# The first mixing of a two-layer network, rebuilt: four-pass products, another order of tiles, masks on the evicted product, long convolution and context FFN behind the recurrence

## The chip, the core and the metric

The kernel runs on one core of a Trainium2 chip. The time is the device time of one execution in microseconds. Before the change three executions took 2928.12, 2919.17 and 2926.59 us; the median is 2926.59. The engines are named as in the profile: PE is TensorE with PEld for its weight loads, DVE is VectorE, ACT is ScalarE, POOL is GpSimd, SP is SyncE, which issues the transfers.

## What is computed

One sequence of 256 tokens with 1024 features, and a context of 256 tokens. Cut to the part that the change touches, the reference does this:

```python
u = rmsnorm(x, mix_norm) @ w_in0                 # 1024 -> 3328 columns
y_r = rwkv7_bidir(u[..., :1792], ...)            # 8 heads of 64, both directions, a scan over 256 steps
y_h = hyena_bidir(u[..., 1792:], ...)            # long convolution through FFTs of 512 points
x = x + concat([y_r, y_h]) @ w_o0                # 512 + 512 -> 1024
# of the second block, which needs nothing of the first mixing:
mod = silu(cond) @ w_mod                         # shift, scale and gate vectors
ctx = ctx + gate * half_ffn(modulated_norm(ctx)) # the context's first half FFN
# then two convolved FFNs, two embeddings, a neighbourhood attention, and the rest of the second block
```

In the recurrence the state of a head is 64 x 64. At each step it is multiplied by a decay, loses its product with a key, and gains an outer product of value and key.

## The kernel before

All is kept feature major: 128 features on the partitions, 256 tokens along the free axis, eight such tiles for H, the residual stream.

A **product** of the kind `gemm` (L351 to L359) is done in three parts. ACT rounds a weight tile to a high part `wh` (L348), DVE or POOL subtracts it from the tile to make the low part `wl` (L349), and the activations are split alike. Each tile of 128 contracted features then has three products of 128x256 in fp32r: high by high (L357), low by high (L358), high by low (L359). Products with fp32 operands that are not split exist too, in the filters and transforms of the long convolution (L763, L783) and in the recurrence. The trace records such a product twice.

**First mixing** (`mix`, L792). The projection takes 26 tiles of columns, eight tiles of the contraction each, in the order of the columns: 0 to 3, 4 to 7 and 8 to 11 for the recurrence's r, k and v by quarter, 12 for decay and rate, 13 for the gate, 14 to 25 for the long convolution. Beside it run the modulation's tiles (`mod_until`, L897): a tile `wm` is 512 KB, DVE sums its product with one conditioning vector (L920), POOL multiplies it with the other (L924) and ACT sums that (L925); 24 tiles are done in the mixing, with two buffers. After tile 13 the first quarter of the recurrence is prepared. Then come the filters of the convolution (their net is three small layers with a Sin each, L704 to L714), the convolution, the solution of the first quarter, the context's norm, and for j = 1 to 3 `prepare(j)` and `solve(j)`. Last are the two halves of the output product (`out0`): the convolution's half is added to H behind the convolution, the recurrence's half at the end (L884).

**A quarter of the recurrence** is two heads in both directions, in eight chunks of 64 steps. `prepare` (L1437) makes decays, keys and values. `solve` (L1514) forms the products G inside the chunks, inverts I + N in blocks of 1, 2, 4 to 32, carries the states along the chunks, and makes the outputs. In the inversion X is the inverse and Y its transpose. Each level multiplies G by the level's mask (L1564, on POOL, one operation for each head's 64 partitions, into `Lv`), forms Lv times X by sixteen 64x64 products (L1557) that ACT copies to `Tm` (L1569), and from two more such batches DVE subtracts in X and Y (L1574, L1575). The first level makes Y and X from the mask alone (L1566, L1567). Behind the last level ACT copies the product that starts the states, W (L1578). Tiles carry the tags `a` and `b` in turn, by quarter.

**The context's first half FFN** needs only the modulation and the context. It is a generator (`half_ffn_on`) that gives its products the tag `fill`. Four of its steps belong to the mixing, the others are handed out after the next phases. Its `wl` is made on POOL as long as the tag is `fill` (L347).

The program is written as Python loops. A scheduler with a timeline model then fixes the order of instructions on each engine when the program is built; transfers marked with `keep_in_program_order` keep theirs. Each engine runs its own list in order, and waits for semaphores of the others. Behind the mixing follow `ffn0`, whose first products are those of L368 to L370 with the tag `mm`, then `ple0` and the rest, in both programs alike.

## Time and profile before

| | before |
|---|---|
| median of three executions | 2926.59 us |
| profiled execution, its span | 2921.7 us |
| PE, DVE, ACT, POOL busy | 95%, 69%, 44%, 24% |
| mean granted TensorE clock | 0.959 |
| traffic | 415.95 MB, 142 GB/s |

The profiled execution is not one of the three that are timed; its span, from the first to the last instruction, stands 4.9 us below their median. "Granted clock" is the share of full speed that PE had in a stretch. A timeline row gives the start, the length, the engine, the line, the operation, what it writes and reads, the size, how many were put together, and in brackets the idle time before it with what ended it. A row of the waits names the waiting instruction, what released it, the sum, how often, and the longest.

The whole span in 40 slices of 73 us, in tenths, shows that the first seven slices differ from the rest:

```
PE   7868999899999989999989999999999999999999
DVE  8896553689977689877764777764756555567555
POOL 3565655322541431241220101000010000121100
PEclk9878999899999999989999999999999999999999
```

### The profile page before, as it was taken

What the parts mean: (1) busy time and instruction counts of PE and PEld (TensorE: products, weight loads), DVE (VectorE), ACT (ScalarE), POOL (GpSimd) and SP (SyncE); (2) the same over time, 40 slices, a digit from 0 to 9 for tenths busy, and PEclk for the clock granted to TensorE, in tenths of its full rate; (3) what the DMA queues carried; (4) which work ended last, traced back from release to release, by engine and by line L of the source; (5) the groups of instructions that cost most, each with busy time, mean ns of one, the idle gap of its engine ahead of it and who ended that gap; (6) DMA issues with size and microseconds to landing.
All of it is one profiled execution on the core that took longest, in us unless ns stands there. A gap on an engine that the chain in (4) does not pass through costs nothing.

```text
span 2921.7 us, 49795 instructions
## 1 busy us (share of the span) xinstructions
PE 2763.4 (95%) x19770; PEld 2453.5 (84%) x19770; DVE 2010.3 (69%) x3432; ACT 1283.4 (44%) x2241; POOL 694.1 (24%) x448
## 2 busy tenths in 40 slices
PE   7868999899989999989999999999999999999999
PEld 6647888799889899989998669888898888895999
DVE  8896553689977689877764764777756555567555
ACT  5433322465645566555554453322233222355543
POOL 3565655322541431241220101000010000121100
PEclk9878999899999999989999999999999999999999
DMA  6421112466555376546641203665535444240554
GB/s 233 154 95 59 55 57 77 160 232 211 174 156 169 104 232 207 179 159 222 213 145 62 65 15 113 195 193 176 167 109 166 139 140 136 76 121 30 169 186 144
DMA packets 145882, 415.95 MB, mean 142 GB/s; under 512 B 31009, under 2 KB 49074, under 8 KB 144754
## 3 DMA queue, kind: packets, MB, share of 16 engines
q1 hardware_dynamic: 144930, 407.52, 43.8%
q0 software_dynamic: 720, 5.24, 0.5%
q8 instruction: 156, 2.56, 0.4%
q14 instruction: 76, 0.62, 0.1%
HBM read 411.66 MB, written 1.05 MB: 141 GB/s over the span
## 4 chain that ended last, share of the span: by engine, by line
PE 64%; DVE 5%; ACT 2%; issue 1%; POOL 0%; DMA 0%; SPq 0%; ACTq 0%; DVEq 0%; POOLq 0%
PE mm L359 17%; PE mm L357 17%; PE mm L358 17%; PE mm L1309 2%; PE mm L369 2%; PE mm L370 2%; PE mm L368 1%; DVE wl L349 1%; PE mm L1277 1%; PE aux L421 1%; PE aux L1303 1%; ACT wh L348 1%; PE fill L359 1%; PE fill L357 1%; PE fill L358 0%
## 5 line engine op out<-in xcount | busy, mean ns | idle before, releaser
L348 ACT CAST wh<-raw 128x1024 fp32r<-128x1024 f32 (+4 forms) x694 | 643.7, 935 | 1011.2 <-PE mm L358 569.2
L349 DVE TENSOR_TENSOR wl<-raw,wh 128x1024 fp32r<-128x1024 f32 (+4 forms) x552 | 690.3, 1254 | 292.6 <-ACT wh L348 283.7
L359 PE MATMUL mm<-xnh,wl 128*128 128x256 f32 (+1 forms) x2592 | 819.0, 316 | 2.1 <-DVE wl L349 2.1
L357 PE MATMUL mm<-xnh,wh 128*128 128x256 f32 (+1 forms) x2592 | 818.3, 316 | 0.7 <-ACT wh L348 0.7
L358 PE MATMUL mm<-xnl,wh 128*128 128x256 f32 (+1 forms) x2592 | 816.2, 315 | 0.0
L359 PEld LDWEIGHTS mm<-xnh,wl 128*128 128x128 f32 x2592 | 488.1, 188 | 35.7 <-DVE wl L349 3.2
L357 PEld LDWEIGHTS mm<-xnh,wh 128*128 128x128 f32 x2592 | 487.8, 188 | 35.7 <-issue 2.3
L358 PEld LDWEIGHTS mm<-xnl,wh 128*128 128x128 f32 x2592 | 487.8, 188 | 34.0
L358 PE MATMUL mm<-ml,wh 128*128 128x256 f32 (+1 forms) x1104 | 341.0, 311 | 6.7 <-DVE ml L349 6.7
L359 PE MATMUL mm<-mh,wl 128*128 128x256 f32 (+1 forms) x1104 | 341.3, 312 | 0.0
L357 PE MATMUL mm<-mh,wh 128*128 128x256 f32 (+1 forms) x1104 | 338.6, 312 | 0.5 <-ACT mh L348 0.5
L349 POOL TENSOR_TENSOR wl<-raw,wh 128x1024 fp32r<-128x1024 f32 (+3 forms) x142 | 257.2, 1819 | 296.9 <-ACT wh L348 246.4
L920 DVE CUSTOM_DVE_ANT_0 junk<-wm,sc,vecs 128x1024 bf16<-128x1024 f32 x224 | 292.2, 1304 | 6.1 <-DMA wm<-w_mod 2.5
L458 POOL TENSOR_TENSOR ss<-ss,xt 128x256 f32<-128x256 f32 x68 | 68.1, 1006 | 917.3 <-issue 690.0
L924 POOL TENSOR_TENSOR wm<-wm,sc 128x1024 f32<-128x1024 f32 x64 | 176.0, 2750 | 438.4 <-DVE mod L920 335.5
L358 PEld LDWEIGHTS mm<-ml,wh 128*128 128x128 f32 x1104 | 207.8, 188 | 21.0 <-DVE ml L349 7.9
L359 PEld LDWEIGHTS mm<-mh,wl 128*128 128x128 f32 x1104 | 207.4, 188 | 12.3
L357 PEld LDWEIGHTS mm<-mh,wh 128*128 128x128 f32 x1104 | 205.6, 188 | 13.2 <-ACT mh L348 0.9
L1003 DVE SCALAR_TENSOR_TENSOR H<-mm,mod,H 128x256 f32<-128x256 f32 x112 | 53.7, 482 | 116.8 <-PE mm L359 116.7
L1050 DVE TENSOR_TENSOR sg<-sg,mm 128x256 f32<-128x256 f32 (+1 forms) x88 | 48.7, 553 | 123.1 <-PE mm L359 120.8
L369 PE MATMUL mm<-xnl,wh 128*128 128x256 f32 x416 | 121.9, 300 | 7.9 <-DVE xnl L954 4.6
L370 PE MATMUL mm<-xnh,wl 128*128 128x256 f32 x416 | 120.2, 296 | 0.0
(539 smaller groups left out, 4738.3 us busy)
## 6 DMA issues: line engine op xcount, KB each, us to landing
raw<-s_up SPq DMA_DIRECT2D x220, 512.0 KB, 3.7
wm<-w_mod SPq DMA_DIRECT2D x144, 512.0 KB, 4.4
raw<-f_up SPq DMA_DIRECT2D x88, 512.0 KB, 4.5
raw<-s_dn SPq DMA_DIRECT2D x65, 512.0 KB, 3.6
raw<-w_in SPq DMA_DIRECT2D x60, 512.0 KB, 3.8
raw<-s_dn SPq DMA_DIRECT2D x60, 384.0 KB, 3.2
raw<-w_o SPq DMA_DIRECT2D x32, 512.0 KB, 3.7
raw<-f_dn SPq DMA_DIRECT2D x32, 512.0 KB, 4.2
```

Of the source, the lines that this page charges most:

```text
L348: self.nc.scalar.copy(hi, src)
L349: (self.nc.gpsimd if pool or self.tag == "fill" else self.nc.vector).tensor_sub(lo, src, hi.bitcast(F32))
L357: nc.tensor.matmul(out, wh[:, ws], h, start=first and k == 0, stop=False)
L358: nc.tensor.matmul(out, wh[:, ws], l, start=False, stop=False)
L359: nc.tensor.matmul(out, wl[:, ws], h, start=False, stop=last and k == kt - 1)
L369: nc.tensor.matmul(out, wh[:, s], l, start=False, stop=False)
L370: nc.tensor.matmul(out, wl[:, s], h, start=False, stop=k == kt - 1)
L458: nc.gpsimd.tensor_add(self.ss[s], self.ss[s], x)
L920: self.tc.keep_in_program_order(nc.vector.tensor_tensor_reduce(out=junk, in0=w, in1=self.sc[:, i], scale=0.5 if self.half else 1.0, scalar ...
L924: nc.gpsimd.tensor_mul(w, w, self.sc[:, 1])
L1003: nc.vector.scalar_tensor_tensor(self.HH[s][:, m], ps[:, c], gt, self.HH[s][:, m], op0=ALU.mult, op1=ALU.add)
L1309: nc.tensor.matmul(po[64 * h : 64 * h + 64, :T], v(k0 // P + i), pTs[h][:, i], start=i == 0, stop=i == nk // P - 1)
```

## The change

- The projection and the output product are no longer split. [...]
- The projection follows what the recurrence needs: tiles 12, 4, 0, 8, then `prepare(0)`, 13, `solve(0)`, then 5, 1, 9, `prepare(1)`, then all others; the filter net is written before the projection, the filters after it. Then `solve(1)`, quarters 2 and 3, the convolution with its half of the output, and the other half.
- The level mask multiplies the product as DVE evicts it (L1600 of the changed file); G itself goes into the product. POOL's masks and ACT's copy are gone.
- In `prepare` five operations go from POOL to DVE. The low parts in the mixing's fill come from DVE.
- Modulation, the context's norm and the context's FFN stand behind the recurrence and the output. For the modulation's 24 tiles both sums run on DVE (`aid=False`).
- The pool `nrm` has three buffers in place of two; the comments are gone, so line numbers differ.

The core of the diff:

```diff
-        (self.nc.gpsimd if pool or self.tag == "fill" else self.nc.vector).tensor_sub(lo, src, hi.bitcast(F32))
+        (self.nc.gpsimd if pool or self.own and self.tag == "fill" else self.nc.vector).tensor_sub(lo, src, hi.bitcast(F32))
...
+    def plain(self, out, w, kt, x):
+        for k in range(kt):
+            self.nc.tensor.matmul(out, w[:, k * P : (k + 1) * P], x[:, k], start=k == 0, stop=k == kt - 1)
...
-                        order = list(range(14)) + [14 + 4 * j + q for q in range(4) for j in range(3)]
-                        for t, wh, wl in self.wtiles("w_in0", order, KT):
...
-                            self.gemm(ps, wh, wl, KT, xh, xl)
...
-                            if t > 1:
-                                self.mod_until(t//3)
...
+                        net = self.filter_net(yp)
...
+                        project([12, 4, 0, 8])
+                        ready = prepare(0)
+                        project([13])
+                        solve(0, ready)
+                        project([5, 1, 9])
+                        ready = prepare(1)
+                        project([6, 2, 10, 7, 3, 11] + [14 + 4 * j + q for q in range(4) for j in range(3)])
+                        kr, ki, hn = self.filters(hp, yp, *net)
+                    rk.pools.append(self.pool(e2, "rke"))
+                    solve(1, ready)
+                    for j in range(2, 4):
+                        solve(j, prepare(j))
+                    self.tag = self.aux = "fill"
+                    self.hyena(x0, sv, kr, ki, hn)
+                self.out0(0, y)
+                fp = self.pool(ef, "fill", side="right")
+                with ExitStack() as e3:
+                    self.mod_open(self.pool(e3, "mod", side="right"), aid=False, eng=nc.sync)
                     self.mod_until(12)
...
+                nc.sync.dma_start(self.HH[1], self.ap["ctx"])
                 for k in range(KT):
                     self.sq_add(k, 1)
                 normed = self.norm2(fp, 0, 0, [1])
...
-        nc.gpsimd.tensor_scalar(lw, lw, 1.0, -0.5 * DECAY, op0=ALU.add, op1=ALU.mult)
+        nc.vector.tensor_scalar(lw, lw, 1.0, -0.5 * DECAY, op0=ALU.add, op1=ALU.mult)
...
-        for lev in range(6):
-            lv = t(pool, [P, 8, 64], "Lv", bufs=2)
-            for h, p in enumerate(PAR):
-                m = self.lmask[p, lev * 64 : lev * 64 + 64].unsqueeze(1).to_broadcast([64, 8, 64])
-                nc.gpsimd.tensor_mul(lv[p], G[p, :, h, 0:64], m)
...
-            nc.scalar.copy(Tm, batch(lambda u, h: lv[PAR[h], u], lambda u, h: X[PAR[h], u]))
+        for lev in range(1, 6):
+            m = self.lmask[:, lev * 64 : lev * 64 + 64].unsqueeze(1).to_broadcast([P, 8, 64])
+            nc.vector.tensor_mul(Tm, batch(lambda u, h: G[PAR[h], u, h, 0:64], lambda u, h: X[PAR[h], u]), m)
```

The order on the engines, at three places. First PE at the start of the program, before; `xnh` and `xnl` are the split norm, `a` the sums of the projection:

```order
L416 MATMUL b_137<-c_sums_64,x_27_120 128x2 x4
L442 MATMUL b_160<-c_ident_66,rsyb_147 128x128 x2
L357 MATMUL a_203<-xnh_163,wh_199 128x256
L357 MATMUL a_235<-xnh_163,wh_231 128x256
L358 MATMUL a_203<-xnl_164,wh_199 128x256
L359 MATMUL a_203<-xnh_163,wl_200 128x256
```

And PE at the same place now; L718 is the filter net, `hy` its layers, L381 the plain product, L1487 belongs to `prepare(0)`:

```order
L438 MATMUL fill_151<-c_sums_64,x_32_131 128x2 x4
L464 MATMUL fill_174<-c_ident_66,rsyfill_161 128x128 x2
L718 MATMUL fill_190<-feat_188,hw_186 64x256
L718 MATMUL fill_202<-hy_192,hw_186 64x256
L718 MATMUL fill_214<-hy_204,hw_186 64x256
L381 MATMUL fill_228<-xn_177,raw_226 128x256 x8
L381 MATMUL fill_240<-xn_177,raw_238 128x256 x8
L381 MATMUL fill_252<-xn_177,raw_250 128x256 x8
L1487 MATMUL b_297<-wa_274,wdec_281 128x256
```

The three products of the filter net stand ahead of the first plain product, and the recurrence's preparation follows after three tiles of the projection.

PE in the levels of a middle quarter, before; `fill` is the context's FFN, L1557 a batch of the inversion:

```order
L357 MATMUL fill_4185<-xnh_2249,wh_4188 128x256
L1557 MATMUL a_2617<-xyt_2459 64x64 x16
L1557 MATMUL a_2634<-xyt_2459 64x64 x16
L358 MATMUL fill_4185<-xnl_2250,wh_4188 128x256
L359 MATMUL fill_4185<-xnh_2249,wl_4189 128x256
L1557 MATMUL a_2656<-xyt_2459,Lv_2653 64x64 x16
```

And in the same levels now; L1586 is the batch, L1631, L1620 and L1624 the states of the quarter ahead, L381 the output product of the convolution:

```order
L1586 MATMUL b_1989<-xyt_1966,G_1918 64x64 x6
L381 MATMUL fill_3086<-sr_3019,raw_3084 128x256 x4
L381 MATMUL fill_3092<-sr_3019,raw_3084 128x256 x4
L1620 MATMUL a_1698<-S_1683,ar_987 64x64 x4
L1586 MATMUL b_2007<-xyt_1966 64x64 x16
L1586 MATMUL b_2024<-xyt_1966 64x64 x3
L1624 MATMUL a_1699<-Lv_1664,xyt_1389 64x64 x4
L1586 MATMUL b_2024<-xyt_1966 64x64 x13
L381 MATMUL fill_3100<-sr_3019,raw_3098 128x256 x3
```

Where the context's FFN stood between the batches, the states of the quarter ahead and the convolution's output stand now.

DVE at the end of the mixing, before; `H` with `a` is the last half of the output product, L386 the root of H's norm:

```order
L884 TENSOR_TENSOR H_59<-H_59,a_5282 128x256
L884 TENSOR_TENSOR H_59<-H_59,a_5303 128x256
L884 TENSOR_TENSOR H_59<-H_59,a_5326 128x256
L349 TENSOR_TENSOR wl_5394<-raw_5391,wh_5393 128x1024
L884 TENSOR_TENSOR H_59<-H_59,a_5347 128x256
L349 TENSOR_TENSOR wl_5406<-raw_5403,wh_5405 128x1024
L386 TENSOR_SCALAR rsxaux_5420<-aux_5415 128x2
```

And DVE there now; L949 is the reduce of a modulation tile `wm`, two for each tile:

```order
L913 TENSOR_TENSOR H_59<-H_59,fill_3155 128x256
L913 TENSOR_TENSOR H_59<-H_59,fill_3164 128x256
L349 TENSOR_TENSOR wl_3463<-raw_3460,wh_3462 128x1024
L913 TENSOR_TENSOR H_59<-H_59,fill_3175 128x256
L913 TENSOR_TENSOR H_59<-H_59,fill_3184 128x256
L949 ISA junk_3203,mod_73<-wm_3201,sc_3198,vecs_58 128x1024
L949 ISA junk_3205,mod_73<-wm_3201,sc_3198,vecs_58 128x1024
L949 ISA junk_3209,mod_73<-wm_3207,sc_3198,vecs_58 128x1024
L949 ISA junk_3211,mod_73<-wm_3207,sc_3198,vecs_58 128x1024
```

The modulation's reduces, which stood among the rows of the projection, follow the last add to H. 32 of them come before the rows of the context's norm, 16 stand between these.

## Rows read from the trace of the kernel before

**Rows 1.** Timeline of PE: start us, us, engine, line, operation, out<-in, count
```profile
561.83 0.28 PE L358 MATMUL fill<-xnl,wh 128*128 128x256 f32 x1
561.95 0.52 PE L368 MATMUL mm<-xnh,wh 128*128 128x256 f32 x3
```

**Rows 2.** Page, engines: busy us, share of the span, instructions
```profile
PE 2763.4 (95%) x19770; PEld 2453.5 (84%) x19770; DVE 2010.3 (69%) x3432; ACT 1283.4 (44%) x2241; POOL 694.1 (24%) x448
```

**Rows 3.** By stage: length; busy PE, PEld, DVE, ACT, POOL; PEclk, DMA, GB/s
```profile
120.00:180.00 60.00, 46.20 (x263) 35.30 (x261) 57.24 (x82) 31.16 (x59) 40.29 (x25) 0.89 0.47 159
180.00:200.00 20.00, 7.45 (x128) 6.94 (x128) 19.88 (x20) 3.81 (x8) 16.37 (x7) 0.57 0.09 27
...
256.00:490.00 234.00, 218.43 (x2706) 185.44 (x2706) 124.03 (x246) 70.48 (x134) 125.40 (x89) 0.89 0.19 56
...
542.00:560.00 18.00, 8.49 (x38) 7.82 (x39) 9.56 (x16) 5.46 (x7) 11.74 (x5) 0.62 0.86 317
```

**Rows 4.** Waits of PE, 0 to 560 us: total, times, longest
```profile
PE b L442 <- DVE rsyb L403: 13.1, 4, 4.8
```

**Rows 5.** Timeline of PE, the first product of the projection
```profile
16.66 0.80 PE L357 MATMUL a<-xnh,wh 128*128 128x256 f32 x2 [1.01 <-ACT xnh L348]
```

**Rows 6.** Timeline of DVE, the first norm and the first filter round
```profile
15.70 0.87 DVE L478 SCALAR_TENSOR_TENSOR xt<-H,vecs,b 128x256 f32<-128x256 f32 x2 [0.79 <-PE b L442]
...
23.45 0.54 DVE L708 TENSOR_SCALAR hy<-fill,vecs 64x256 f32<-64x256 f32 x1 [0.94 <-PE fill L704]
...
24.66 0.87 DVE L712 SCALAR_TENSOR_TENSOR hy<-hn__227_1306,hy 64x256 f32<-64x256 f32 x2
```

**Rows 7.** Timeline of PE, products of the projection in a row
```profile
36.19 0.28 PE L358 MATMUL a<-xnl,wh 128*128 128x256 f32 x1
36.31 0.28 PE L359 MATMUL a<-xnh,wl 128*128 128x256 f32 x1
```

**Rows 8.** Timeline of PE, plain products of the inverse transform (L783)
```profile
214.99 1.03 PE L783 MATMUL fill<-c_dfti,st 128*128 128x256 f32 x4
215.85 1.03 PE L783 MATMUL fill<-c_dfti,kr 128*128 128x256 f32 x4
```

**Rows 9.** DVE's lines, 0 to 250 us: busy us, mean ns, idle before
```profile
L349 DVE TENSOR_TENSOR wl<-raw,wh 128x1024 fp32r<-128x1024 f32 x20 | 25.6, 1280 | 5.0 <-ACT wh L348 5.0
...
L1435 DVE SCALAR_TENSOR_TENSOR v<-zs,vecs,v 128x256 f32<-128x256 f32 x6 | 11.1, 1894 | 0.0
```

**Rows 10.** By stage, instructions of the tile fill on PE alone
```profile
256.00:490.00 234.00, 88.60 (x571) 0.89 0.19 56
...
490.00:542.00 52.00, 18.42 (x130) 0.87 0.30 96
```

**Rows 11.** Line L1578, the copy that makes W, one per quarter
```profile
L1578 ACT COPY Lv<-b x2: 587/588/588, 249.3 to 408.6; 128x512 f32<-128x512 f32 x2
L1578 ACT COPY Lv<-a x2: 587/587/587, 330.4 to 490.3; 128x512 f32<-128x512 f32 x2
```

**Rows 12.** Line L1567, X before the levels, second and fourth quarter
```profile
L1567 DVE TENSOR_TENSOR xyt<-c_eye,a x2: 675/682/689, 272.1 to 437.4; 128x512 f32<-128x512 f32 x2
```

**Rows 13.** Timeline of DVE, the last add to H of the mixing
```profile
541.80 0.41 DVE L884 TENSOR_TENSOR H<-H,a 128x256 f32<-128x256 f32 x1
```

**Rows 14.** Line L1564, the level masks on POOL, and who waits
```profile
L1564 POOL TENSOR_TENSOR Lv<-G,c_lmask x48: 1252/1286/5476, 173.5 to 471.6; 64x512 f32<-64x512 f32 x48
...
  PEld b L1557: 7.0, 2
```

**Rows 15.** DVE's lines, 256 to 490 us: busy, mean ns, idle
```profile
L1574 DVE TENSOR_TENSOR xyt<-xyt,a 128x512 f32<-128x512 f32 x8 | 5.5, 687 | 23.5 <-PE a L1557 23.5
...
L952 DVE SCALAR_TENSOR_TENSOR xt<-Hc,mod,fill 128x256 f32<-128x256 f32 x8 | 3.5, 472 | 0.3 <-PE fill L442 0.3
```

**Rows 16.** Tile wm, 0 to 250 us: the reduces' ns min/median/max
```profile
L920 DVE CUSTOM_DVE_ANT_0 junk<-wm,sc,vecs x24: 1265/1273/2819, 36.9 to 233.8; 128x1024 bf16<-128x1024 f32 x24
```

**Rows 17.** DMA issues, 0 to 250 us: count, KB each, median us to landing
```profile
wm<-w_mod SPq DMA_DIRECT2D x24, 512.0 KB, 3.6
```

More of the change, by code (lines that the diff above doesn't have):

```diff
@@ L359, in gemm, with plain_tiles @@
             nc.tensor.matmul(out, wl[:, ws], h, start=False, stop=last and k == kt - 1)
+    def plain_tiles(self, name, todo):
+        arr = self.ap[name]
+        i = 0
+        while i < len(todo):
+            t, k0, kn = todo[i]
+            n = kn * P
+            m = 1
+            while i + m < len(todo) and (m + 1) * n <= 1024 and todo[i + m] == (t + m, k0, kn):
+                m += 1
+            raw = self.t(self.raw, [P, 1024], "raw")
+            src = arr[t : t + m, :, k0 * P : k0 * P + n].rearrange("t p n -> p t n")
+            self.nc.sync.dma_start(raw[:, : m * n].rearrange("p (t n) -> p t n", t=m), src)
+            for j in range(m):
+                yield t + j, raw[:, j * n : (j + 1) * n]
+            i += m
+    def plain(self, out, w, kt, x):
+        for k in range(kt):
+            self.nc.tensor.matmul(out, w[:, k * P : (k + 1) * P], x[:, k], start=k == 0, stop=k == kt - 1)
     def gemm_wide(self, outs, ws, kt, xh, xl, cols=slice(0, T)):
@@ L682, in na, with filter_net, filters @@
                 self.sq_add(m)
-    def filters(self, pool):
+    def filter_net(self, tp):
+        nc = self.nc
+        w = self.t(tp, [64, 1216], "hw")
+        nc.sync.dma_start(w, self.ap["hy_w"])
+        feat = self.t(tp, [17, T], "feat")
+        nc.sync.dma_start(feat, self.ap["hyfeat"])
+        p64 = slice(0, 64)
+        x, kdim = feat, 17
+        for j in range(3):
+            ps = self.acc("aux")
+            nc.tensor.matmul(ps[p64, :T], w[:kdim, 64 * j : 64 * j + 64], x[:kdim], start=True, stop=True)
+            y = self.t(tp, [64, T], "hy", bufs=2)
+            n = self.t(tp, [64, T], "hn_")
+            f = self.vec("hfreq", 0, p64)
+            nc.vector.tensor_scalar(y, ps[p64, :T], self.vec(f"hb{j + 1}", 0, p64), f, op0=ALU.add, op1=ALU.mult)
+            nc.vector.tensor_scalar(n, y, 1.0 / (2 * math.pi), 12582912.0, op0=ALU.mult, op1=ALU.add)
+            nc.vector.tensor_scalar(n, n, -12582912.0, None, op0=ALU.add)
+            for c in (6.28125, 0.0019350051879882812, 3.019916050561733e-07):
+                nc.vector.scalar_tensor_tensor(y, n, -c, y, op0=ALU.mult, op1=ALU.add)
+            nc.vector.tensor_scalar(y, y, -math.pi, math.pi, op0=ALU.max, op1=ALU.min)
+            nc.scalar.activation(y, y, AF.Sin)
+            x, kdim = y, 64
+        return x, w
+    def filters(self, pool, tp, x, w):
         nc = self.nc
@@ L777, in hyena @@
             nc.vector.tensor_copy(kr[0:1, 0], ny[:, 1])
-            yh, yl = (self.t(pool, [P, 4, T], n, F32R) for n in ("sr", "si"))
+            out = self.t(pool, [P, 4, T], "sr")
             for q in range(4):
@@ L855, in mix @@
-                    self.tag = self.aux = "fill"
-                    for _ in hy:
-                        pass
-                fp = self.pool(ef, "fill", side="right")
+                        self.tag = self.aux = "fill"
+                        r = self.rows(sq[::2], T, "all", 1.0 / D)
+                        xn = self.t(tp, [P, KT, T], "xn")
+                        for k in range(KT):
+                            nc.vector.scalar_tensor_tensor(xn[:, k], self.H[:, k], self.vec("mix_norm", k), r,
+                                                           op0=ALU.mult, op1=ALU.mult)
@@ L861, in mix @@
                 normed = self.norm2(fp, 0, 0, [1])
-                rk.pools.append(self.pool(e2, "rke"))
-                for j in range(1, 4):
-                    self.tag = self.aux = "ba"[j % 2]
-                    rk.solve(j, rk.prepare(j))
-                self.tag = self.aux = "fill"
                 self.rest = self.half_ffn_on(fp, 0, 0, [1], FILL, normed=normed)
```

126 lines of the change are left out of this document (47 added, 79 removed).

## The prediction

> **What bounds the kernel now.** I read the views in this order: the page, a table by stage over the first 560 us, the waits of PE in that stretch, and the lines that carry a price. The change ends where the latent tokens' first FFN begins, for behind that product both programs issue the same work. In the trace of before it starts at 561.95 us [rows 1]; the row above it is the last of the context's FFN ("fill"). So the question is when this product starts afterwards; what lies behind it, some 2360 us, I take as unchanged.
>
> The page says PE 95% busy [rows 2], an average over stages of different kinds. The table by stage [rows 3] shows what hides in it: from 256 to 490 us PE is busy 218.43 of 234 us, since the context's FFN fills the gaps of the recurrence; in 120:180 it is busy 46.20 of 60, in 180:200 7.45 of 20 at a granted clock of 0.57 while DVE is busy 19.88, and in 542:560 8.49 of 18 at 0.62. Ahead of the recurrence's middle, then, DVE and POOL set the pace, inside it PE. The waits are short: the largest sum over 560 us is 13.1 us [rows 4]. No single wait is to be freed; work must go, or move.
>
> **The start.** The first product of the projection now waits for the filter net, whose three small products stand ahead of it on PE, two of them behind a DVE chain and a Sin. In before the first product starts at 16.66 us [rows 5]. Its successor waits for the norm's eight rows (two take 0.87, so 3.5 us from 15.70) and for two rounds of the net (0.54 for the first of its operations, 0.87 for two of the three alike [rows 6], three more and Sin: with hand-overs I estimate 3.5 to 4 us each), so about 26 us: +9. It can hardly be below +5, since the chain runs on one engine; if the norm's sums come late it is +12.
>
> **Plain products.** 816 products of the split kind go, 272 plain ones come. A split product takes 0.117 us from start to start [rows 7]; four records of the plain kind, which are two products (each leaves two), take 0.86 us [rows 8], so 0.43 each. 816 x 0.117 = 95.5 us against 272 x 0.43 = 117: +21.5 us of PE at full clock. With the splits go 20 DVE operations (25.6 us before 250 us [rows 9]), as many casts on ACT and those on POOL; the modulation's 24 reduces (over 30 us of DVE [rows 16]) leave this stretch too. So the projection becomes bound by PE: 208 x 0.43 = 89 us, one quarter of the recurrence, and the filter's products, 16 of 128x512 among them (twice 0.43 each, 14 us). A quarter's own PE work comes from the recurrence stretch: 218.43 less the fill's 88.60 [rows 3, 10] is 129.8 us in 234 us, so 44.6 per period of 80.3 (below), and 40 at full clock. 89 + 40 + 14, with the second preparation and small products (about 14), is 157; from 26 that ends near 183, and the second quarter's X is made at about 190. In before it is made at 272.1 [rows 12]: 82 us are gained by here, of which the PE time that stood idle before pays most.
>
> **The recurrence.** W copies run from 249.3 to 490.3 us over four quarters [rows 11]: three periods of 80.3 us. In each the fill takes 88.60 / 2.91 = 30.4 us of PE [rows 10]; without it 50 remain. The hyena convolution now lies in these gaps: 32 plain products of its output and 32 of the inverse transform (13.8 us each), and 16 of 128x512 (14), 41 us over three quarters. The level masks leave POOL (1.29 us median, 48 of them [rows 14]) for one DVE operation at the eviction, 0.688 by the row of the same shape [rows 15]. Bounds of that edit: the waits on POOL that end are 7.0 us in all [rows 14], a DVE queue that stands longer could cost as much; I take zero. The products that go from POOL to DVE in a preparation (five of 128x512, 3.4 us a quarter) lie beside PE work in the middle quarters. I take 60 us a period, 50 and most of a third of the 41: the first W of the second quarter at 190 + 53 = 243 (before: 330.4 less 272.1, 58, with 20 of fill in it, here with 15 of hyena), then 304 and 363. The tail from W was 51.5 us in before (490.3 to the last add to H at 541.80 [rows 13]), with 18.4 of fill [rows 10]; its chain of states waits on itself, so less than half of the fill comes off: 44, the last add at 407. Bounds: 379 with periods of 48, 435 with periods of 68.
>
> The granted clock is 0.89 in the filled recurrence and 0.57 where PE is thinly busy [rows 3]; 0.57 lies near the lower of its two levels, 0.89 near the upper. [...] By the row of 0.89 the sum stands; were the quarters at the lower level throughout, each would need (40 + 14) / 0.5 = 108 us and the whole some 3080 us. [...]
>
> **What is late next.** Here the cover is gone. In before the 24 modulation tiles lay beside the projection, and the context's FFN inside the recurrence. Afterwards DVE has the modulation's reduces behind the last add to H, and the context's norm behind 32 of them; PE has nothing until then. Two reduces per tile at 1.27 us make 2.5; a tile lands 3.6 us after its issue [rows 16, 17]. With two buffers a buffer turns in 2.5 + 0.3 + 3.6 = 6.4 us, so a tile each 3.2; the first two are there already. Queued behind them on SP are all later transfers, further weights of the FFN among them. Tile 16 is done 51 us after the last add. The norm's eight steps alternate with the other 16 reduces on DVE, about 4.4 us for each two: it ends at +70, and the first four FFN tiles (96 products) at +86. The other 674 of 770 products follow at 0.117 us: 79 us, with stalls for splits 84. The latent FFN starts at 407 + 170 = 577, against 562. Bounds of this stretch: 150 (2.5 a tile, no stall) and 190 (first products at the low level, late splits).
>
> **Sum.** +15 at the marker; 770 context products stand ahead of it where 740 did, and these 30 (3.5 us) come off behind it: +11.5. The profiled execution's span is 2921.7; the median of the runs, 2926.6, is 4.9 above it. 2921.7 + 11.5 + 4.9 = 2938.
>
> **Rivals.**
> (a) Faster: with POOL out of the levels DVE speeds up and the period falls to 48. For it: DVE operations beside POOL run long, as the mix of v at 1.894 us [rows 9] where another of the same operation and shape takes 0.472 [rows 15]. [...] Against it: in the levels DVE waits for PE (23.5 us [rows 15]), not the other way. Last add at 379, 28 earlier: 2910.
> (b) Slower still: without dense fill the clock stays between its levels, about 0.75, and 54 us of a period become 68 and more. For it: 0.57 and 0.62 [rows 3]. Against it: the level chain has a batch of products every microsecond or so. Last add at 435: 2966. It decides from a granted clock under 0.8 in the middle quarters.
> (c) No change: with periods of 55 the last add comes at 393, and what is gained ahead of it is just paid back by the stretch of 170: marker at 563, 2924.
> (d) The plain product costs more than 0.43 beside other work, 0.5: 272 x 0.07 = +19, 2957.
>
> **Chances.** Forecast 0.42 (own range 2926 to 2954), (a) 0.26, (b) 0.12, (c) 0.14, (d) 0.06. A measurement of this kernel cannot tell less than 0.3%, 8.8 us, from no change. Faster comes from (a) and the early edge of (c): 0.27. Within 0.3%: most of (c) and the low edge of the forecast: 0.23. Slower: 0.50. The range for 8 in 10 reaches from below (a) to past (b): 2898 to 2976.
>
> **What would show it.** Right: the first plain product at about 26 us; four records per 0.86 us in the projection; the second quarter's X at about 190; W copies about 60 us apart; the last add near 407; then some 50 us with PE idle, DVE in reduces and a w_mod transfer each 3.2 us; the first latent FFN product near 577. Wrong: the last add before 395, where the gain wins; reduces that run ahead of it; or the marker after 600.

## The result, and the profile after

The changed kernel is slower by 1%: the ratio of its times to those of the kernel before is 1.0107, with a 95% interval of 1.0080 to 1.0134 (median 2958.17 us against 2922.88). Three of its four executions agree (2950.30, 2958.17 and 2960.74 us) and are the ones compared; the fourth took 3934.77 us at a mean granted clock of 0.643 and is left out. The profiled execution is the first of the three, with a span of 2948.2 us, 26.5 more than before. It is the fastest of them, so a time in its trace may stand up to 10 us earlier than in another execution. The engines' line of its page, the answer to [rows 2]:

```profile
PE 2764.2 (94%) x19498; PEld 2439.7 (83%) x19498; DVE 1978.7 (67%) x3518; ACT 1210.7 (41%) x2116; POOL 426.0 (14%) x284
```

PE is as busy as before; POOL has lost 268 us of work.

The same table by stage as in [rows 3], now in slices of 30 us (window; length; busy PE, PEld, DVE, ACT, POOL; granted clock, DMA share, GB/s):

```profile
0.00:30.00 30.00, 11.33 (x35) 7.87 (x36) 16.26 (x53) 4.50 (x9) 0.20 (x4) 1.00 0.69 231
30.00:60.00 30.00, 30.00 (x144) 23.93 (x143) 14.06 (x36) 14.46 (x31) 0.00 (x0) 1.00 0.36 112
...
120.00:150.00 30.00, 30.00 (x350) 25.53 (x346) 9.84 (x18) 3.67 (x7) 1.46 (x2) 1.00 0.32 99
...
300.00:330.00 30.00, 22.34 (x184) 16.29 (x183) 18.89 (x47) 4.73 (x11) 0.72 (x1) 0.59 0.10 36
...
360.00:390.00 30.00, 23.37 (x332) 18.37 (x328) 7.59 (x19) 1.67 (x5) 0.00 (x0) 0.67 0.01 2
...
420.00:450.00 30.00, 2.55 (x10) 2.07 (x10) 24.26 (x45) 2.08 (x5) 8.19 (x6) 0.50 0.46 141
450.00:480.00 30.00, 3.52 (x11) 2.64 (x12) 26.46 (x47) 1.82 (x4) 0.00 (x0) 0.50 0.50 159
480.00:510.00 30.00, 23.31 (x141) 22.05 (x140) 27.01 (x47) 11.62 (x18) 4.79 (x2) 0.72 0.60 190
510.00:540.00 30.00, 29.23 (x236) 28.44 (x235) 20.79 (x33) 12.39 (x21) 1.09 (x1) 1.00 0.62 198
```

From 30 to 150 us PE has no idle time and the full clock (1.00 in each of the four slices), where before DVE and POOL held it ([rows 3], 120 to 180). From 420 to 480 PE is busy 6 of 60 us at a granted clock of 0.50, while DVE is busy 51: that hole did not exist before. Its walls are on PE's timeline (start, length, engine, line, operation, in brackets the idle time before and what ended it):

```profile
26.09 12.08 PE L381 MATMUL fill<-xn,raw 128*128 128x256 f32 x48
...
400.92 13.27 PE L381 MATMUL fill<-y,raw 128*128 128x256 f32 x52 [1.05 <-DVE y L1663]
428.64 1.01 PE L438 MATMUL fill<-c_sums,ss 128*128 128x2 f32 x4 [14.45 <-POOL ss L480]
...
444.52 0.69 PE L464 MATMUL fill<-c_ident,rsyfill 128*128 128x128 f32 x2 [14.02 <-DVE rsyfill L425]
473.63 0.58 PE L357 MATMUL fill<-xnh,wh 128*128 128x256 f32 x1 [28.42 <-ACT xnh L982]
...
600.01 0.64 PE L390 MATMUL mm<-xnh,wh 128*128 128x256 f32 x4
```

The first plain product comes at 26.09 us, where the split one came at 16.66 ([rows 5]); the 48 records in its row are 24 products, since each leaves two. The first latent product comes at 600.01, against 561.95 [rows 1]. What DVE did in the hole (its timeline, same columns):

```profile
414.22 0.42 DVE L913 TENSOR_TENSOR H<-H,fill 128x256 f32<-128x256 f32 x1 [0.75 <-PE fill L381]
418.41 1.28 DVE L949 CUSTOM_DVE_ANT_0 junk<-wm,sc,vecs 128x1024 bf16<-128x1024 f32 x1 [3.77 <-ACT sc L937]
...
436.84 1.28 DVE L949 CUSTOM_DVE_ANT_0 junk<-wm,sc,vecs 128x1024 bf16<-128x1024 f32 x1 [0.81 <-DMA wm<-w_mod]
...
462.01 1.28 DVE L949 CUSTOM_DVE_ANT_0 junk<-wm,sc,vecs 128x1024 bf16<-128x1024 f32 x1 [0.44 <-DMA wm<-w_mod]
...
465.20 1.28 DVE L949 CUSTOM_DVE_ANT_0 junk<-wm,sc,vecs 128x1024 bf16<-128x1024 f32 x1 [0.57 <-DMA wm<-w_mod]
...
470.94 0.17 DVE L960 TENSOR_SCALAR mod<-mod 128x16 f32<-128x16 f32 x1
```

The last add to H ends at 414.6 ([rows 13]: 541.80 before). Then 32 reduces run to 470.94, where the scale vectors are finished (L960) and the norm can begin. The tile `wm` over that stretch (ns min/median/max, first and last start), the answer to [rows 16, 17]:

```profile
L949 DVE CUSTOM_DVE_ANT_0 junk<-wm,sc,vecs x48: 1274/1284/1619, 418.4 to 499.7; 128x1024 bf16<-128x1024 f32 x48
...
  DMA wm<-w_mod: 6.5, 12
...
DMA to landing us min/median/max: 3.4/3.5/3.7
```

A reduce takes 1.28 us, with the read of its sum 1.33 (from one start to the next, 443.10 to 444.43), so 2.66 a tile. DVE waited 6.5 us in all for these transfers: from 443 us on each tile waits 0.4 to 0.8 us for its own, and a tile comes every 3.0 to 3.2 us. So most of the pace is the reduces, and the rest is the turn of the two buffers. W and X of the quarters ([rows 11, 12] before), line L1609 and the tile `xyt`:

```profile
L1609 ACT COPY Lv<-b x2: 565/576/586, 142.7 to 305.0; 128x512 f32<-128x512 f32 x2
L1609 ACT COPY Lv<-a x2: 585/585/585, 253.0 to 367.9; 128x512 f32<-128x512 f32 x2
```

```profile
L1595 DVE TENSOR_TENSOR xyt<-c_eye,a x2: 686/686/686, 199.7 to 337.0; 128x512 f32<-128x512 f32 x2
```

So 128 us are gained up to the last add (541.8 to 414.2), and the stretch from there to the first latent product grows from 20 to 186: 166 lost. Behind that product 11.6 us come back (2348.2 us to the end, 2359.8 before).

### The profile page after: what moved, and what is told of

The parts are those of the page before. It is cut to its first block, busy times and chain, and to the rows that moved or that the text cites. A ratio compares the mean times of both kernels' runs of the same rounds, so it can differ in the third digit from the quotient of the medians.

```text
span 2948.2 us, 48945 instructions
## 1 busy us (share of the span) xinstructions
PE 2764.2 (94%) x19498; PEld 2439.7 (83%) x19498; DVE 1978.7 (67%) x3518; ACT 1210.7 (41%) x2116; POOL 426.0 (14%) x284
## 4 chain that ended last, share of the span: by engine, by line
PE 62%; DVE 6%; ACT 1%; issue 1%; DMA 1%; SPq 0%; POOL 0%; ACTq 0%; DVEq 0%; POOLq 0%
PE mm L357 17%; PE mm L359 17%; PE mm L358 16%; PE mm L1338 2%; PE mm L391 2%; DVE wl L349 2%; PE mm L392 2%; PE mm L390 1%; PE mm L1306 1%; PE aux L443 1%; PE aux L1332 1%; ACT wh L348 1%; DVE xt L981 0%; PE fill L357 0%; PE fill L358 0%
## 5 line engine op out<-in xcount | busy, mean ns | idle before, releaser
L348 ACT CAST wh<-raw 128x1024 fp32r<-128x1024 f32 (+4 forms) x652 | 607.0, 938 | 972.4 <-PE mm L358 553.9
L349 DVE TENSOR_TENSOR wl<-raw,wh 128x1024 fp32r<-128x1024 f32 (+3 forms) x568 | 705.8, 1246 | 306.7 <-ACT wh L348 297.9
L949 DVE CUSTOM_DVE_ANT_0 junk<-wm,sc,vecs 128x1024 bf16<-128x1024 f32 x248 | 320.0, 1290 | 14.6 <-DMA wm<-w_mod 6.5
L359 PEld LDWEIGHTS mm<-mh,wl 128*128 128x128 f32 x1104 | 207.2, 188 | 13.7 <-DVE wl L349 0.4
L480 POOL TENSOR_TENSOR ss<-ss,xt 128x256 f32<-128x256 f32 x68 | 74.0, 1094 | 993.0 <-issue 689.6
L349 POOL TENSOR_TENSOR wl<-raw,wh 128x1024 fp32r<-128x1024 f32 (+2 forms) x84 | 156.8, 1873 | 351.6 <-ACT wh L348 254.4
L953 POOL TENSOR_TENSOR wm<-wm,sc 128x1024 f32<-128x1024 f32 x40 | 111.8, 2795 | 367.0 <-DVE mod L949 302.0
L357 PE MATMUL fill<-xnh,wh 128*128 128x256 f32 x352 | 107.0, 304 | 42.8 <-ACT xnh L982 30.6
```

The source lines that it names most:

```text
L348: self.nc.scalar.copy(hi, src)
L349: (self.nc.gpsimd if pool or self.own and self.tag == "fill" else self.nc.vector).tensor_sub(lo, src, hi.bitcast(F32))
L357: nc.tensor.matmul(out, wh[:, ws], h, start=first and k == 0, stop=False)
L359: nc.tensor.matmul(out, wl[:, ws], h, start=False, stop=last and k == kt - 1)
L480: nc.gpsimd.tensor_add(self.ss[s], self.ss[s], x)
L949: self.tc.keep_in_program_order(nc.vector.tensor_tensor_reduce(out=junk, in0=w, in1=self.sc[:, i], scale=0.5 if self.half else 1.0, scalar ...
```

## The experiments

All were timed in three rounds. The ratio is to the kernel before; 1.0107 is the change itself. "Norm" is the start of DVE's first row of the latent tokens' norm ahead of their first FFN, "second block" the start of the first norm row of the second block. The places come from one profiled execution of each kernel, the ratios from several.

| kernel | time, us | ratio, interval | second quarter's W | last add | norm | second block |
|---|---|---|---|---|---|---|
| before | 2922 to 2925 | 1 | 330.4 | 541.8 | 559.2 | 1305.7 |
| changed | 2958 | 1.0107 (1.0080 to 1.0134) | 253.0 | 414.2 | 595.2 | 1332.9 |
| mods_early | 2940 | 1.0066 (1.0041 to 1.0090) | 247.8 | 451.1 | 581.7 | 1319.5 |
| mods_first | 2915 | 0.9969 (0.9956 to 0.9982) | 260.4 | 426.2 | 554.7 | 1293.2 |
| old_stages | 2910 | 0.9956 (0.9943 to 0.9969) | 328.4 | 538.9 | 556.6 | 1295.6 |
| stages_first | 2886 | 0.9864 (0.9848 to 0.9881) | 300.5 | 507.7 | 525.2 | 1269.7 |
| a_split | 2953 | 1.0104 (1.0078 to 1.0131) | 248.6 | 406.5 | 591.6 | 1329.2 |
| a_masks | 2969 | 1.0151 (1.0136 to 1.0166) | 259.9 | 424.4 | 608.8 | 1353.0 |
| a_net | 2968 | 1.0164 (1.0137 to 1.0191) | 258.9 | 425.4 | 608.4 | 1350.4 |
| a_warm | 2968 | 1.0152 (1.0122 to 1.0181) | 255.7 | 422.6 | 603.3 | 1348.4 |
| b_plain | 2907 | 0.9942 (0.9927 to 0.9957) | 312.7 | 525.9 | 543.7 | 1295.0 |
| b_masks | 2940 | 1.0053 (1.0036 to 1.0069) | 311.0 | 545.7 | 560.6 | 1318.5 |
| best1 | 2901 | 0.9930 (0.9910 to 0.9951) | 323.3 | 522.6 | 540.5 | 1278.5 |
| best2 | 2917 | 0.9987 (0.9975 to 0.9999) | 341.0 | 539.8 | 557.5 | 1294.9 |

**mods_early: the modulation beside the projection.**

```diff
                         project([12, 4, 0, 8])
+                        self.mod_open(mp, aid=False, eng=nc.sync)
...
+                                done += 1
+                                if done > 4:
+                                    self.mod_until((done - 2) // 2)
...
-                    self.mod_open(self.pool(e3, "mod", side="right"), aid=False, eng=nc.sync)
-                    self.mod_until(12)
-                self.nrm = self.pool(e2, "nrm", bufs=3)
+                self.nrm = self.pool(e2, "nrm", bufs=2)
```

> The changed kernel with the 24 modulation tiles taken back beside the projection (both sums on DVE as in the change), the context's norm and FFN still behind the output product; one buffer fewer in the pool of the norm's squares. Theory: the change loses because DVE's 48 reduces, about 57 us from 414 to 471 with PE idle, stand in line behind the last add to H; beside the projection DVE was busy only 14 to 21 of each 30 us, so they hide there. Then the last add stays within 10 us of 414, the first latent FFN product comes at about 548 in place of 600, and the time falls by about 50, to some 2900 us, below the kernel before. Rival 1 (the plain products' 21 us of PE are the loss): no more than 10 us of change, since PE's work is the same. Rival 2 (the reduces only move): they delay the recurrence's preparation by as much as they free, last add at 450 or later, time above 2935.

It gained about 12 us (1.0107 to 1.0066), not 50. From the last add to the norm it is 131 us in place of 181, so the 50 were saved; but the last add came 37 later, as the second rival has it, and the first latent product at 586, not 548. The queue of SP shows why (its timeline: start, length of the group, line, what is loaded):

```profile
66.57 73.53 SPq L373 DMA_DIRECT2D raw<-w_in  x14
143.22 15.42 SPq L373 DMA_DIRECT2D raw<-w_o  x4
205.42 0.34 SPq L1553 DMA_DIRECT2D gup<-g_up  x1
209.94 7.45 SPq L948 DMA_DIRECT2D wm<-w_mod  x3
```

The order of that queue put 20 of the 24 modulation tiles behind the projection's weights, whose loads, with the output's, waited for PE 26 times, 119.0 us in all up to 330, and behind a small load that waited 46.8 us for a product; DVE's order put the reduces there too. So they fell in one block into the recurrence:

```profile
120.00:150.00 30.00, 30.00 (x356) 25.48 (x356) 10.76 (x21) 3.96 (x7) 1.46 (x2) 1.00 0.36 107
...
210.00:240.00 30.00, 15.69 (x258) 13.39 (x256) 28.81 (x59) 2.35 (x5) 0.00 (x0) 0.66 0.49 146
240.00:270.00 30.00, 19.26 (x182) 15.82 (x178) 29.75 (x57) 6.17 (x12) 0.00 (x0) 0.66 0.34 106
```

DVE is at 10.76 of 30 us where the reduces were meant to be, and full where the levels need it; PE falls to 15.69 at 0.66.

**mods_first: the same, written ahead of the first quarter's preparation, transfers on POOL's queue.**

```diff
-                                    self.mod_until((done - 2) // 2)
...
                         self.mod_open(mp, aid=False, eng=nc.sync)
+                        self.mod_until(12)
...
-                self.tc.keep_in_program_order(nc.sync.dma_start(w, self.ap[f"w_mod{l}"][t]))
+                self.tc.keep_in_program_order((nc.sync if self.tag == "mm" else nc.gpsimd).dma_start(w, self.ap[f"w_mod{l}"][t]))
```

> As the run with the modulation beside the projection, but its 24 tiles are written ahead of the first quarter's preparation and their transfers go through POOL's queue, so that DVE's order spreads the 48 reduces over the rows of the first quarter and the projection, in place of one block behind it (there they stood at 205 to 300 us with DVE 28 of 30 us busy, and held the second quarter). Theory (the reduces are free where PE works from its own queue, and cost their length where DVE is on the chain): the last add returns from 451 to about 420, the first latent product comes at about 550, time about 2903. Rival (they cost their length wherever they stand, since the first quarter's chain waits for DVE as well): last add at 445 or later, 2935 or more.

The last add is at 426, near the expected 420, and the first latent product at 560, not 550; the time is 2915, 12 above what was expected, and 0.3% below the kernel before. Taken out of the tail the reduces save 52 us there (181 to 128.5) and cost 12 ahead of it. The place in the program and the queue were changed together, so the run doesn't say which of the two did it. The norm comes 40.5 us earlier than in the changed kernel. DVE now has its full stretch beside the projection, and PE keeps 27 of 30 us and its clock:

```profile
90.00:120.00 30.00, 27.41 (x198) 22.83 (x199) 29.81 (x64) 8.22 (x18) 4.90 (x7) 1.00 0.60 197
120.00:150.00 30.00, 27.38 (x324) 22.13 (x326) 29.04 (x57) 6.06 (x11) 3.71 (x7) 1.00 0.59 186
```

**old_stages and stages_first: the stages in the old order.** Convolution and its output half before the second quarter, the context's norm next, its FFN in the gaps of the recurrence, the last output half at the end; modulation as in mods_early and as in mods_first.

```diff
-                    solve(1, ready)
-                    for j in range(2, 4):
-                        solve(j, prepare(j))
                     self.tag = self.aux = "fill"
+                    nc.sync.dma_start(self.HH[1], self.ap["ctx"])
                     self.hyena(x0, sv, kr, ki, hn)
-                self.out0(0, y)
...
                 normed = self.norm2(fp, 0, 0, [1])
...
+                solve(1, ready)
+                for j in range(2, 4):
+                    solve(j, prepare(j))
+                self.tag = self.aux = "fill"
                 self.rest = self.half_ffn_on(fp, 0, 0, [1], FILL, normed=normed)
                 for _ in range(CUT):
                     next(self.rest)
+                self.tag, self.aux = "a", "b"
+                self.out0(0, y)
```

> The changed kernel with the stages in the old order behind the projection: modulation beside the projection, convolution with its output half before the second quarter's solution, the context's norm next, its FFN handed to the gaps of quarters 2 to 4, the last output half at the end; plain products, the new order of tiles, masks at the eviction stay. Theory: PE is then full in the recurrence again, with periods of about 80 us from a first X near 200, and there is no serial stretch: last add at about 480, marker at about 500, time about 2855 us. Rival 1 (plain products are the loss): above 2900. Rival 2 (early modulation delays the first quarters by its 64 us of DVE): marker about 550, time about 2905.

> As the run with the old order of stages, with the modulation's tiles written ahead of the first quarter's preparation and their transfers on POOL's queue. In the run before, DVE was 28 to 30 of 30 us busy from 240 to 330 and the second quarter's W came at 328. Theory: without that block W of the second quarter comes at about 270, the last add at about 480, and the time is about 2860. Rival (the context's norm and FFN in the recurrence's gaps cost what they save): W as late as 310, last add after 515, time above 2895.

old_stages falls short of the theory: 2910 lies above the 2900 of the first rival and near the 2905 of the second. The trace speaks for the second: the same block of reduces held the second quarter's W until 328; b_plain below answers the first. Without the block stages_first is the fastest kernel of the study, 1.4% below the kernel before, though W came at 300 and not at 270, and the last add at 508 and not at 480, between theory and rival. mods_first differs from it by the place of convolution, context norm and FFN, with the tags of the last output half and the load of the context that go with them. Against it the norm comes 29.5 us earlier: this is what the fill of the gaps is worth. The stage table of stages_first shows it; in mods_first PE is busy 23.13 us at 0.78 and 29.25 at 0.67 in these two slices:

```profile
300.00:330.00 30.00, 30.00 (x536) 26.50 (x531) 15.79 (x32) 5.89 (x11) 0.00 (x0) 1.00 0.20 59
330.00:360.00 30.00, 30.00 (x282) 24.91 (x280) 13.19 (x35) 8.13 (x17) 0.00 (x0) 0.83 0.11 34
```

**a_split: the projection split again.**

```diff
-                            for t, w in self.plain_tiles("w_in0", [(t, 0, KT) for t in tiles]):
-                                self.plain(ps, w, KT, xn)
+                            for t, wh, wl in self.wtiles("w_in0", tiles, KT):
+                                self.gemm(ps, wh, wl, KT, xh, xl)
```

> The changed kernel with the projection's 208 products split again (624 products of the fp32r kind, casts on ACT, low parts on DVE); the output products stay plain. Theory: up to the filters PE sets the pace, and 624 x 0.117 is 16 us less than 208 x 0.43; DVE has room for 26 low parts (33 us) there, so the whole gains up to 16 us at the most: 2940 to 2950. Rival (the splits were what bound this stretch, and plain products are what freed it): W of the first quarters 15 us or more later, time 2965 or more.

The last add comes 7.7 us earlier, the norm 3.6, and the ratio is the same; 2953 lies just above the theory's range and well below the rival's. In the new order the runs show no difference between the two kinds of product in the projection.

**b_plain: the kernel before with plain products alone.**

```diff
-                            self.gemm(ps, wh, wl, KT, xh, xl)
+                            self.plain(ps, wr, KT, xn)
...
-            self.gemm(ps[:, :T], wh, wl, 4, yh, yl)
+            self.plain(ps[:, :T], w, 4, y)
```

> The kernel before with the projection and both output halves as plain products, nothing else. Theory: its first 256 us wait for DVE and POOL, and the splits that go are 26 casts and low parts of the projection and 8 of the outputs; so the time falls by 10 to 30 us (2895 to 2912) although PE has 21 us more. Rival 1 (PE's work decides): 21 us slower, 2945. Rival 2 (the modulation's reduces and POOL hold the stretch, not the splits): within 8 us of before.

17 us less, as the theory had it, with 21 us more of PE by the estimate (its busy time rose by 11.6, from 2763.4 to 2775.0): there the splits were in the way, and PE was not. So the plain products are no part of the loss.

**a_masks and b_masks: the level masks, undone and alone.**

```diff
-            nc.scalar.copy(Tm, batch(lambda u, h: lv[PAR[h], u], lambda u, h: X[PAR[h], u]))
+            nc.vector.tensor_mul(Tm, batch(lambda u, h: G[PAR[h], u, h, 0:64], lambda u, h: X[PAR[h], u]), m)
```

(with the mask on POOL that goes; a_masks has the lines reversed in the changed kernel.)

> The changed kernel with the level masks back on POOL and the copy of the product on ACT, as in the kernel before (the preparation's operations stay on DVE). Theory: the masks are made ahead, so a level waits as long as before; W copies of the middle quarters move by less than 4 us and the time stays within 8 us of the changed kernel (2943 to 2960). Rival (the mask at the eviction shortened the chain): each period grows by 5 x 1.3 us or more, POOL's operations stretch DVE's, and the time is 20 us or more above the changed kernel.

> The kernel before with the level masks at the eviction on DVE (ACT's copy and POOL's masks gone), nothing else. Theory: POOL's 48 operations of 1.3 us and more leave; the first quarter's inversion, which stood at 190 to 249 us with POOL and DVE full, gains 5 to 10 us, the filled quarters nothing; time 5 to 12 us less (2912 to 2919). Rival (PE is full there, so nothing moves): within 4 us.

Both miss. With the masks back on POOL the changed kernel is some 13 us slower (1.0151 against 1.0107, whose intervals just miss each other), between theory and rival; the last add is 10 us later. In the kernel before they make it slower by 0.5%: the second quarter's W comes 19 us earlier (311.0 against 330.4), the last add 4 later and the second block 13 later. The gain was given back in the filled quarters and behind them; 722 context products stand ahead of the latent ones there where 740 did, which explains 2 us. The rest is open: no run took the order behind the mixing as its one difference.

**a_net: the filter net behind the projection's fifth tile.**

```diff
-                        net = self.filter_net(yp)
...
                         project([13])
+                        self.tag = self.aux = "fill"
+                        net = self.filter_net(yp)
```

> The changed kernel with the filter net written behind the projection's tile 13 in place of ahead of the projection, nothing else. Theory: the first plain product comes 9 us earlier, at about 17 us, and since PE is full from there to 180 us all of it is gained: last add at about 405, time about 2946 (9 us below the changed kernel). Rival (the first quarter's chain, which waits for DVE and ACT, sets the stretch): last add within 3 us of 414, no gain.

The first product did come at 13.7 us in place of 26.1 and the first quarter's W at 131.7 in place of 142.7; the time is worse by 0.6%, some 17 us, which neither theory nor rival had. The net's DVE work then falls beside the first preparation, and PE starves there:

```profile
0.00:30.00 30.00, 20.51 (x87) 17.41 (x88) 11.05 (x38) 9.91 (x22) 0.20 (x4) 1.00 0.84 283
30.00:60.00 30.00, 20.61 (x82) 12.91 (x81) 24.71 (x63) 14.34 (x25) 0.00 (x0) 0.68 0.15 44
```

What PE gains in the first 30 us (9.2) it loses in the next (9.4), and X of the second quarter is made at 218.1 in place of 199.7. So the 9 us of the start were not to be had by an earlier start alone.

**a_warm: products that nothing reads, for the clock.**

```diff
+            if j > 1:
+                for n in range(2):
+                    nc.tensor.matmul(psu[:, T:], net.ident, W[:, 4 * n : 4 * n + 4], start=True, stop=True)
```

> The changed kernel with two idle products of 128x256 (four-pass, into columns that nothing reads) in each step of the states of quarters 3 and 4: 16 products, 6.9 us of PE at full clock, at places where PE waited for DVE. In the changed kernel the granted clock was 0.59 to 0.84 from 300 to 420 us. Theory of the low clock: fed with them PE keeps a higher clock there (0.8 and more in each of the slices 300 to 390), and the last add comes 5 to 15 us earlier. Rival (the chain of DVE and PE hand-overs sets the time there, the clock only stretches what waits anyway): the clock rises but the last add stays within 3 us of 414, or comes up to 7 us later.

```profile
300.00:330.00 30.00, 24.69 (x213) 17.03 (x207) 18.93 (x45) 5.73 (x13) 0.72 (x1) 0.64 0.07 28
330.00:360.00 30.00, 28.79 (x320) 23.34 (x322) 10.74 (x28) 3.24 (x8) 0.00 (x0) 0.74 0.03 12
360.00:390.00 30.00, 23.23 (x440) 18.05 (x435) 11.77 (x28) 2.06 (x6) 0.00 (x0) 1.00 0.02 4
```

In one slice the clock rises from 0.67 to 1.00; in the others it goes from 0.59 to 0.64 and from 0.84 to 0.74. The last add comes 8 us later, 2.9 of which stand there at the third quarter's W, before the first added product; the ratios' intervals overlap, and 8 us are within the 10 by which the changed kernel's executions differ. From the last W (375.0) to the last add it is 47.6 us, against 46.3 at a clock of 0.63, with eight of the added products in it; by its slices, 1.00 to 390 and 0.66 from there to 420, its mean clock is 0.76 to 0.79 (an estimate). So a higher clock did not shorten this tail, which speaks for its hand-overs between PE and DVE. The period before it lies for the most part in the slices in which the clock stayed at 0.64 and 0.74, so what it costs there is not shown.

**best1 and best2: what points past the change.** stages_first with the net moved as in a_net, and that with the modulation's second sum on POOL and ACT again.

```diff
-                        self.mod_open(mp, aid=False, eng=nc.sync)
+                        self.mod_open(mp, eng=nc.sync)
```

(This is best2 against best1.)

> The run with the old order of stages and the modulation ahead of the first quarter, with the filter net moved behind tile 13 as well. Theory: as in the changed kernel the first product comes 9 us earlier, but DVE was 29 to 30 of 30 us busy from 90 to 150 us there, so only part of it is kept: 2877 to 2884. Rival: the net's DVE work then lies in the stretch that DVE bounds, and nothing is gained (2886).

> The last one with the modulation's second sum on POOL and ACT again (as in the kernel before), so that DVE has 24 reduces in place of 48 from 50 to 165 us. Theory: DVE's full stretch (90 to 150 us) loses 32 us of reduces, POOL and ACT are nearly idle there, so W of the first quarter returns from 172 towards 145 and PE closes its gaps: 5 to 15 us less than the run without it, 2865 to 2875. Rival (POOL's products stretch DVE's own operations by as much, as in the kernel before): no gain or a loss.

Both are slower than stages_first. With the net moved the first product comes 12 us earlier and the whole is 0.7% slower, much as in a_net. With the sums shared W of the first quarter came at 162.9 in place of 174.2, but the convolution's adds to H moved from 285 to 301 us and the second quarter's W from 323 to 341. Why is not shown.

## Why the prediction was right, and which terms were off

The direction and the mechanism were as forecast: gain ahead of the last add, loss behind it, since the modulation stands on DVE alone with PE idle. The size was too low: 11.5 us were forecast, the profiles say 26.5 and the timed runs 31 (1.07% of 2923). The time of 2958 lies in the wide range, but outside the forecast's own of 2926 to 2954, and the marker at 600.01 lies just past the 600 that was named as a sign of being wrong. By steps:

- **The start**: 26 forecast, 26.09 measured.
- **Plain products**: that PE becomes the bound came true (30.00 of 30 us from 30 to 150), but X of the second quarter is made at 199.7 and not at 190: PE is busy 173 of the 174 us from 26 to there, not 157. Of the 16 more, some 7 lie in the projection, whose 208 products took 96 us in place of 89, and some 7 are the clock, 0.83 from 160 to 199.7 where the sum took full speed (estimates from these figures).
- **The recurrence**: W at 253.0, 305.0 and 367.9, forecast 243, 304 and 363; the tail measured 46.3 and was taken as 44. The last add is only 7 us late, in part by luck: X is 10 late, the two periods are 115 us in place of 120, and the tail is 2 longer. The term behind the 60 was wrong twice. The convolution's share was counted in records, of which each product leaves two: its inverse transform is 16 products of 128x256 and its transform 8 of 128x512, so it is 28 us of PE and not 41. And the periods do not follow the fill. PE in the two periods and in the tail, first all of it, then the tile `fill` alone (columns as in the stage table; the second view has PE, clock and DMA only):

```profile
253.00:305.00 52.00, 49.97 (x726) 40.02 (x722) 22.30 (x54) 6.09 (x15) 0.00 (x0) 0.93 0.22 81
305.00:367.90 62.90, 53.13 (x724) 41.91 (x724) 31.29 (x75) 6.22 (x16) 0.72 (x1) 0.73 0.06 20
367.90:414.20 46.30, 36.74 (x202) 26.77 (x202) 11.98 (x35) 7.92 (x17) 4.75 (x6) 0.63 0.14 45
...
253.00:305.00 52.00, 13.96 (x56) 0.93 0.22 81
305.00:367.90 62.90, 1.13 (x4) 0.73 0.06 20
```

  The period with hardly any fill is the longer one, at the lower clock; the convolution was done by then. The prediction had the fill lengthen a period.
- **What is late next** was mis-sized most: 186 us, not 170. The 16 tiles took 56 (51 forecast), of which 3.8 are the wait for the conditioning vectors' Silu, that was not counted; their pace of 3.0 to 3.2 us a tile was as forecast. The 0.3 in the turn of a buffer was the author's estimate: the two reduces with their reads and the landing, 2.66 and 3.5, are 6.2 of the 6.3 to 6.5 us that two tiles took. The norm went on to 487, +73 (+70). The first 96 products of the FFN were done at 503, +89 (+86): 48 of them by 491, the others behind a wait of 3.1 us, as the last reduces stand between the FFN's rows on DVE, and at a clock of 0.50 from there to 500. The rest is where it failed: the other 674 products were given 84 us, 5 of them for stalls, and took 97 (503 to 600). Waits of PE are 10 of these: 4.5 for the latent tokens' root, 2.9 for a gate, and six short ones. The pace of 0.120 us a product in place of 0.117 and the clock behind the last wait (0.59 from 595 to 600) add some 1.5 us each, by estimate; the rest was not taken apart. The waits on PE's timeline:

```profile
494.35 0.58 PE L357 MATMUL fill<-xnh,wh 128*128 128x256 f32 x1 [3.08 <-DVE sg L1082]
...
591.67 0.43 PE L464 MATMUL aux<-c_ident,rsyaux 128*128 128x128 f32 x2 [4.52 <-DVE rsyaux L425]
595.46 0.55 PE L357 MATMUL fill<-xnh,wh 128*128 128x256 f32 x1 [2.87 <-DVE sg L1083]
```

- **Behind the marker** 3.5 us were to come off, and 11.6 did; where the other 8 come from is not shown.
- The sum: +7 and +16, less 8, is 15 over the forecast of +11.5, which is the 26.5 of the profiles.

Of the rivals, (a) had its premise right and fell all the same: with POOL idle (busy 6.2 us in all up to 400) the mix of v takes 0.48 us, where six of them took 1.89 before ([rows 9]), two of them 5.17 us from 62.66, while POOL was busy from 61.74 to 67.54; but the two periods average 57 us, not 48. The row now:

```profile
L1464 DVE SCALAR_TENSOR_TENSOR v<-zs,vecs,v 128x256 f32<-128x256 f32 x8 | 3.7, 482 | 1.3 <-ACT v L1462 1.3
```

The two levels of the clock that the prediction names are 0.50 and 1.00 in the trace of the kernel before, and 0.50 stands there with PE idle and with PE busy throughout (columns as in the stage table):

```profile
185.00:190.00 5.00, 0.00 (x0) 0.00 (x0) 4.98 (x4) 2.70 (x5) 4.00 (x3) 0.50 0.25 63
...
225.00:230.00 5.00, 4.52 (x54) 3.82 (x51) 3.48 (x7) 2.33 (x5) 3.32 (x4) 1.00 0.30 100
...
375.00:380.00 5.00, 5.00 (x55) 3.89 (x54) 1.73 (x3) 0.42 (x1) 0.00 (x0) 0.50 0.01 3
```

(b) met its condition in part (0.59, 0.84 and 0.67 from 300 to 390), and what it describes is met in the period of 62.9 us at 0.73; but the period before it kept 0.93, and the last add was not at 435. How much of those 62.9 us the clock costs stays open: in a_warm the period took 67.1 us (307.9 to 375.0), most of it at 0.64 and 0.74, and in mods_first 58.7 us, with 0.78, 0.67 and 0.90 in the slices from 300 to 390. (c) needed a last add at 393. (d) comes nearest by its number, 2957, and is excluded by its cause: at full clock the records of plain products stand 0.216 us apart (20 of them take 4.48 us from 29.80), 0.43 a product as reckoned, and a_split and b_plain show no cost of the kind of product. That such a product makes four passes, as the title has it, is not shown: it leaves two records and takes 3.7 times the 0.117 us of a split one. That the loss is the placement and not the parts is shown: with the modulation written first the same parts run at 0.9969, and with the old order of stages as well at 0.9864 (both with two buffers in the pool `nrm` in place of three).

## What to carry to other kernels

Work that hides beside another engine's is cheap only as long as it stands there (in mods_first the reduces cost 12 us ahead of the last add and save 52 behind it): before moving a filler behind the stage it filled, sum what it cost in engine time, since what nothing else covers comes back as a serial stretch (here 56 us until the reduces of 16 tiles are done and 90 of products, 770 x 0.117, of the 166 lost). Look at the clock as well where a filler goes (0.73 in the period without fill, 0.93 in the one with). Where a scheduler orders the instructions, moving a call in the program does not place its work (in mods_early 20 of the 24 tiles came behind the projection's weights): read the order of the queue that loads for it (here SP's) and of the engine that does it, and write the call ahead of what it must precede.

## What was not expected

- An earlier start made the kernel slower: 12 us less until the first product (a_net), and some 17 us more on the whole.
- Two edits that change nothing in the program behind the mixing moved the time behind it by up to 11 us: from the norm to the second block it is 746.5 us in the kernel before, 737.7 in the changed one and 757.9 in b_masks. Each is one execution, and those of the kernel before differ by up to 19 us as a whole (2912.5 to 2931.5), so part of it may be spread.
- Of the five reduces that started while POOL added the context's squares (418.8 to 428.6 us in the changed kernel), four took 1.62 us in place of 1.28 and one 1.29. Why that one was spared is not shown.
